# Every operand of TensorE at a multiple of 256 bytes, and the convolution mixer's end by halves of the tokens

## The chip, the cores and the metric

The kernel runs on one core of a Trainium2 chip. The metric is the time of one execution in microseconds (us) on the device. A core has a matrix engine (TensorE, PE in the profile), three engines that work on whole tiles (VectorE or DVE, ScalarE or ACT, GpSimd or POOL), SyncE (SP), which in this kernel issues nearly all transfers, an on-chip memory of 128 partitions (SBUF) and accumulators for PE in banks (PSUM).

## The reference

A trunk of four layers over 512 tokens of width 1024. Each layer has a token mixer (a Conformer convolution module, HGRN2, mLSTM, stick-breaking attention, in this order) and a gated feed-forward part (FFN) of inner width 2816:

```python
shift1, scale1, gate1, shift2, scale2, gate2 = split(silu(c) @ ada_w[i] + ada_b[i], 6)
h = x * (1 + scale1) + shift1
y = mixer(h)                                     # by layer
x = layer_norm(alpha * x + (1 + gate1) * y)
h = x * (1 + scale2) + shift2
x = layer_norm(alpha * x + (1 + gate2) * conv_ffn(h))

def conformer_conv_module(h):                    # mixer of layer 0
    u = glu(h @ w_pw1 + b_pw1)                   # 1024 -> 2048 -> 1024
    u = causal_dwconv(u, dw_w) + dw_b            # 31 taps, channel by channel
    u = silu(layer_norm(u, ln_g, ln_b))          # over the channels of a token
    return u @ w_pw2 + b_pw2
```

All is in 32-bit floats.

## The kernel before

**Products.** PE multiplies in a rounded 32-bit type (fp32r). To keep the precision each factor is split into a high and a low part, and a product is three matmuls: high by high, low by high, high by low. A weight tile `r_*` of 128x1024 comes by one transfer, ACT casts it to `wh_*` (L252), DVE subtracts to get `wl_*` (L254). Where an output is scaled by the row `gate` (1 + gate1), the raw weights are first multiplied by it on DVE (L242). A matmul has a stationary operand, which PE loads into its array ahead of time, and a moving one of up to 512 columns that streams through. In the products "up" (L282: `p_f`, `p_pw`, `p_mup`, ...) the weights are stationary and the activations `hh`, `hl` move. In the products "down" (L351: `p_d` of the FFN, `p_mdn`, `p_pw`, ...) the activations (`gr0h`, `muh`, `cuh`, ... and the low ones) are stationary and the weights move.

**Where tiles lie.** All tiles live in pools, stacked one behind another in each partition (4 bytes an element). Small tiles (a constant of 1 column, one of 8, statistics of 4 or 12 columns, modulation columns of 48) lie in the same pools as the large ones, and so decide at which byte each large tile begins. In the program before, the weight rings `wh`/`wl` and the activations `hh`/`hl` begin 192 bytes behind a multiple of 256. The FFN's down activations and those of the mLSTM begin 64 behind one, and so do the spare weight tiles with which the last three weight pairs of a down product are kept at once (`tail`, `spare`). The `hh_first` of the first product of the trunk begins 192 behind, its first weights (pool `start`) 224. The mLSTM's `ph`, `pl`, `wh_mv`, `wl_mv` begin at a multiple of 256.

**The conformer.** For each of 8 groups of 128 channels: two up products (`p_pw` L282, value and gate), a sigmoid, the product `upad`; `upad` goes to DRAM (`ud`) and comes back as four shifted copies `R`; 28 of the taps are matmuls (`pc` L681), the others run on DVE (`cv`); the sum (`cv` L689) is transposed to token-major (`ct` L653) and copied into `tm` (ACT), with statistics `cst` on DVE. Then comes the transition. All four blocks of 128 tokens are normalised, transposed back eight times (`cb` L703, 128x512), go through silu (L705, 512 tokens at a time), and are split into `cuh` and `cul` (L325, L326). Then the down product `p_pw` (L351) of 192 matmuls starts, with the gate rows (`gb` L445) just before it, and each bank of it is added to `X` on DVE (L585), which ends the sub-layer and leads to the FFN.

**The order.** PE's order is that of the code, here. On the other engines a list scheduler orders instructions by a priority: weight loads and splits are raised ahead. The modulation (`ada`, L207 and L208) is 48 units for a layer: a transfer of 512 KB on SP, and a multiply-and-sum of 128x1024 on DVE. `fill` puts units between the up products of the conformer (3 for each group), `flush` the rest. A transfer waits in SP's order until its tile is free, and all that stands behind it waits too.

Of the kernel before, what the change touches and what calls it, by code (L numbers as in the profile page):

```python
# [10 lines left out]
F32 = mybir.dt.float32  # L11
# [37 lines left out]
HEAD = 3  # L49

# [89 lines left out]

class Trunk:
    def __init__(self, ctx, tc, ins, out):
# [3 lines left out]
        self.const = E(tc.tile_pool(name="const", bufs=1))  # L146
        self.wp = E(tc.tile_pool(name="wp", bufs=2))
        self.xp = E(tc.tile_pool(name="xp", bufs=1))
        self.sp = E(tc.tile_pool(name="sp", bufs=2))
        self.ps = E(tc.tile_pool(name="ps", bufs=1, space=PSUM))  # L150
# [3 lines left out]
        self.ones = self.const.tile([P, 1], F32, name="ones")  # L154
# [3 lines left out]
        self.mhalf = self.const.tile([P, 8], F32, name="mhalf")  # L158
# [15 lines left out]

    def load_x(self):
        for t in range(NT):
            self.nc.sync.dma_start(out=self.X[t], in_=self.ins["x"][t * P:(t + 1) * P, :])
# [6 lines left out]
    def begin_layer(self, i):  # L184
# [5 lines left out]
        ab = self.sp.tile([P, 48], F32, tag="adab", name=f"adab{i}")  # L190
# [3 lines left out]
        ac = self.sp.tile([P, 48], F32, tag="adac", name=f"adac{i}")  # L194
# [286 lines left out]
    def mod_cols(self, i, which, prev):  # L481
# [10 lines left out]
        GB = self.sp.tile([P, 2 * KD], F32, tag="GB", name=f"GB{i}_{which}")  # L492
# [32 lines left out]
    def first_h(self, i, w=None, us=(), name=None):  # L525
# [5 lines left out]
        with tc.tile_pool(name="start", bufs=1, side="right", reuse_waits="tile") as st:  # L531
# [19 lines left out]
    def sub_end(self, ep, i, which, nxt, bias=None, gate=None, due=True):  # L551
# [22 lines left out]
        def evict(h, t, ps, partial=False):  # L574
# [7 lines left out]
            if h == 0:  # L582
                st[t] = self.sp.tile([P, 2, 6], F32, tag="st", bufs=4, name=f"st_{name}_{t}")
# [22 lines left out]
    def rstd(self, st, name):  # L606
        nc = self.nc
        mv = self.sp.tile([P, 4], F32, tag="mv", bufs=4, name=f"mv_{name}")
# [18 lines left out]
    def conformer(self, nxt):  # L627
# [9 lines left out]
        with tc.tile_pool(name="cf", bufs=1, reuse_waits="tile") as op, ExitStack() as es, \  # L637
                tc.tile_pool(name="cd", bufs=1, space=bass.MemoryType.DRAM) as dr:
# [4 lines left out]
            cf = es.enter_context(tc.tile_pool(name="cg", bufs=1, reuse_waits="tile"))  # L643
# [47 lines left out]
            self.flush(i, 40)  # L691
            self.apool = None
            es.close()
            cf = es.enter_context(tc.tile_pool(name="ch", bufs=1, reuse_waits="tile"))
# [12 lines left out]
            bias = cf.tile([P, D], F32, name="bpw2")  # L707
            nc.sync.dma_start(out=bias, in_=ins["bpw2"].broadcast_to([P, D]))
            gate, evict = self.sub_end(cf, i, 0, nxt, bias)
            act = self.ring(cf, us, "cu", keep=True)  # L710
            self.down(ins["pw2"], KD, act, "pw2", 2, evict, tail=TAIL, gate=gate,
                      spare=lambda tag, nm: cf.tile([P, D], F32R, tag="tw", bufs=4, name=nm))


    def hgrn(self, nxt):
# [4 lines left out]
        with tc.tile_pool(name="hg", bufs=1, reuse_waits="tile") as op, ExitStack() as es:  # L720
            og = [op.tile([P, T], F32, name=f"og{k}") for k in range(H)]
            ng = op.tile([P, 1], F32, name="hng")
            nc.sync.dma_start(out=ng, in_=ins["hng"])
            vs = es.enter_context(ExitStack())
            vp = vs.enter_context(tc.tile_pool(name="hv", bufs=1, side="right", reuse_waits="tile"))
            hp = es.enter_context(tc.tile_pool(name="hh", bufs=1, reuse_waits="tile"))
# [74 lines left out]
            def decay(hd, Q, F, K, G):  # L801
# [6 lines left out]
                ex = hp.tile([P, 3, NC], F32, tag="ex", bufs=2, name=f"ex{hd}")  # L808
# [16 lines left out]
            def mix(hd, stag, QP, KP, QD, KD_, dec):  # L825
# [48 lines left out]
                ms = hp.tile([P, 8], F32, tag="ms", bufs=2, name=f"ms{hd}")  # L874
# [56 lines left out]
            late["p"] = es.enter_context(tc.tile_pool(name="hw", bufs=1, side="right", reuse_waits="tile"))  # L931
# [5 lines left out]
    def mlstm(self, nxt):  # L937
# [7 lines left out]
        with tc.tile_pool(name="mx", bufs=1, reuse_waits="tile") as mp, \  # L945
                tc.tile_pool(name="md", bufs=1, space=bass.MemoryType.DRAM) as dr:
            xc = [mp.tile([P, T], F32, name=f"xc{m}") for m in range(NM)]
            with tc.tile_pool(name="ma", bufs=1, reuse_waits="tile") as ap:
                vd = [dr.tile([2, P, D], F32, name=f"mvd{h}") for h in range(H)]
                Sr = [ap.tile([P, 1280], F32, name=f"Sr{h}") for h in range(H)]  # L950
                self.psum(mm="012", at="34", sm="5", tr="67")
# [9 lines left out]
                msel = ap.tile([P, 8], F32, name="msel")  # L961
                nc.sync.dma_start(out=msel, in_=ins["msel"])
                bg = ap.tile([4, 2], F32, name="mbg")
# [25 lines left out]
                for hd in range(H):  # L989
# [4 lines left out]
                    for q in range(4):  # L994
# [12 lines left out]
                        bd = ap.tile([P, 32 + 4 * P], F32, tag="bd", bufs=1, name=f"bd{m}")  # L1007
# [52 lines left out]
                gb = ap.tile([P, 32 + 4 * P], F32, tag="bd", bufs=1, name="gb")[0:4, 0:T]  # L1060
# [92 lines left out]
    def stick(self, nxt):  # L1153
# [3 lines left out]
        with tc.tile_pool(name="so", bufs=1, reuse_waits="tile") as op, ExitStack() as es:  # L1157
# [134 lines left out]
            late["p"] = es.enter_context(tc.tile_pool(name="sf", bufs=1, reuse_waits="tile"))  # L1292
            self.psum(mm="234501", tr="67")
            for _ in dn:
                pass
# [85 lines left out]
```

## Time and profile before

| | |
|---|---|
| time, median of 3 runs | 2715.64 us (2715.63 to 2717.45) |
| the profiled execution | 2719.89 us, its span 2718.1 us |
| PE busy | 2620.6 us, 96% of the span, 13012 matmuls and transposes |
| DVE, ACT, POOL busy | 1991.0 us (73%), 1192.1 us (44%), 43.3 us (2%) |
| transfers | 352.66 MB, mean 130 GB/s |
| granted clock, mean | 0.987 |

The span is the profiled time without its start and end. PE's clock has two levels, 1.2 and 2.4 GHz; a granted clock of 1.00 is the upper one. A line of the profile such as L351 is a line of the kernel before. A matmul's duration in the profile overlaps with the next matmul, so the distance from one start to the next (the pitch) says what a matmul costs in a full stream, and a mean duration shows differences between groups. PE is full nearly everywhere. The stretch in which it is not is the conformer, up to 255 us, and its end above all.

### The profile page before, as it was taken

How to read it: one execution, taken by the hardware profiler on the slowest of the kernel's cores; microseconds unless marked ns; L12 is line 12 of the kernel's file. 1: busy time of each engine (PE TensorE's matmuls, PEld its weight loads, DVE VectorE, ACT ScalarE, POOL GpSimd, SP SyncE). 2: the span in 40 equal slices, each digit the busy share in tenths (PEclk: the TensorE clock that was granted, in tenths of full speed). 3: DMA queues.
4: the chain of work that ended last, by engine and by line, in shares of the span. 5: the costliest groups of instructions: out<-in, count | busy, mean ns of one | idle time of the engine just before them, and what ended most of it. 6: DMA issues, size and time to landing. Idle time of an engine off the chain costs nothing.

```text
span 2718.1 us, 33772 instructions
## 1 busy us (share of the span) xinstructions
PE 2620.6 (96%) x13012; PEld 2099.0 (77%) x13012; DVE 1991.0 (73%) x3051; ACT 1192.1 (44%) x1750; POOL 43.3 (2%) x80
## 2 busy tenths in 40 slices
PE   7979999999998999999999999999999999999998
PEld 5537888887876788888887778888887776888886
DVE  7558997775677799666766777898676577766676
ACT  3124433334774443334555543543434454543332
POOL 0000000000000000000000000000000000000000
PEclk9989999999998999999999999999999999999999
DMA  8843874232221386223222223675323311323232
GB/s 318 242 115 129 299 246 155 97 115 90 86 67 51 114 300 229 93 97 107 87 90 73 86 78 116 211 266 167 101 93 98 96 55 47 101 94 116 93 97 74
DMA packets 109529, 352.66 MB, mean 130 GB/s; under 512 B 12088, under 2 KB 22328, under 8 KB 109368
## 3 DMA queue, kind: packets, MB, share of 16 engines
q1 hardware_dynamic: 109368, 350.50, 39.2%
q8 instruction: 102, 1.67, 0.2%
q14 instruction: 59, 0.48, 0.1%
HBM read 341.96 MB, written 8.50 MB: 129 GB/s over the span
## 4 chain that ended last, share of the span: by engine, by line
PE 81%; DVE 8%; ACT 5%; DMA 3%; issue 2%; POOL 1%; SPq 0%; POOLq 0%; DVEq 0%; ACTq 0%
PE p_f L282 35%; PE p_d L351 16%; PE p_mup L282 6%; PE p_mdn L351 3%; PE p_hqf L282 2%; PE p_sqk L282 2%; PE p_pw L282 2%; PE p_hv L351 1%; PE p_sv L351 1%; PE p_pw L351 1%; DMA ada<-in_ada_dram 1%; PE ms L981 1%; ACT hf L515 1%; PE p_hg L282 1%; DMA r_swo<-in_swo_dram 1%
## 5 line engine op out<-in xcount | busy, mean ns | idle before, releaser
L282 PE MATMUL p_f<-hl,wh_f 128*128 128x512 f32 (+1 forms) x1504 | 565.4, 376 | 1.2 <-DVE hl L522 1.2
L282 PE MATMUL p_f<-hh,wl_f 128*128 128x512 f32 (+1 forms) x1504 | 564.8, 376 | 0.0
L282 PE MATMUL p_f<-hh,wh_f 128*128 128x512 f32 (+1 forms) x1504 | 564.1, 376 | 0.0
L252 ACT CAST wh_f<-r_f 128x1024 fp32r<-128x1024 f32 x176 | 185.0, 1052 | 340.8 <-PE p_f L282 308.3
L282 PEld LDWEIGHTS p_f<-hl,wh_f 128*128 128x128 f32 x1504 | 283.1, 188 | 53.0 <-DVE hl L522 1.6
L282 PEld LDWEIGHTS p_f<-hh,wh_f 128*128 128x128 f32 x1504 | 282.6, 188 | 52.2 <-ACT hh L521 0.9
L282 PEld LDWEIGHTS p_f<-hh,wl_f 128*128 128x128 f32 x1504 | 283.0, 188 | 51.0 <-issue 0.2
L254 DVE TENSOR_TENSOR wl_f<-r_f,wh_f 128x1024 fp32r<-128x1024 f32 x176 | 214.9, 1223 | 136.3 <-ACT wh_f L252 135.8
L208 DVE CUSTOM_DVE_ANT_0 ada<-ada,sbc,adab 128x1024 f32<-128x1024 f32 x192 | 243.4, 1278 | 8.3 <-DMA ada<-in_ada_dram 8.3
L1312 DVE SCALAR_TENSOR_TENSOR cv<-p_f,par,cv 128x511 f32<-128x511 f32 (+1 forms) x176 | 131.1, 745 | 1.4
L1312 DVE SCALAR_TENSOR_TENSOR cg<-p_f,par,cg 128x511 f32<-128x511 f32 (+1 forms) x176 | 131.1, 745 | 1.3
L242 DVE TENSOR_TENSOR r_d<-r_d,gate 128x1024 f32<-128x1024 f32 x88 | 107.5, 1222 | 27.7 <-DMA r_d<-in_fdn_dram 26.7
L1322 ACT ACTIVATE cg<-cg 128x512 f32<-128x512 f32 x88 | 55.4, 629 | 162.2 <-DVE cg L1312 162.2
L254 DVE TENSOR_TENSOR wl_d<-r_d,wh_d 128x1024 fp32r<-128x1024 f32 x88 | 107.4, 1221 | 11.3 <-ACT wh_d L252 11.3
L282 PE MATMUL p_mup<-hh,wh_mup 128*128 128x512 f32 (+1 forms) x280 | 108.4, 387 | 0.9 <-ACT hf L515 0.9
L282 PE MATMUL p_mup<-hh,wl_mup 128*128 128x512 f32 (+1 forms) x280 | 107.1, 382 | 0.0
L282 PE MATMUL p_mup<-hl,wh_mup 128*128 128x512 f32 (+1 forms) x280 | 106.6, 381 | 0.0
L252 ACT CAST wh_d<-r_d 128x1024 fp32r<-128x1024 f32 x88 | 92.3, 1048 | 20.0 <-PE p_f L282 16.0
L624 ACT ACTIVATE X<-X,mv 128x512 f32<-128x512 f32 x56 | 43.1, 810 | 82.0 <-DVE mv L612 82.0
L1310 ACT ACTIVATE cg<-p_f,par 128x512 f32<-128x512 f32 x88 | 68.1, 774 | 13.8 <-PE p_f L282 13.8
L351 PE MATMUL p_d<-wl_d,gr0h 128*128 128x512 f32 x176 | 69.6, 396 | 0.0
L351 PE MATMUL p_d<-wl_d,gr2h 128*128 128x512 f32 x176 | 69.6, 396 | 0.0
(469 smaller groups left out, 5619.5 us busy)
## 6 DMA issues: line engine op xcount, KB each, us to landing
ada<-in_ada_dram SPq DMA_DIRECT2D x192, 512.0 KB, 4.8
r_f<-in_fup_dram SPq DMA_DIRECT2D x176, 512.0 KB, 3.7
r_d<-in_fdn_dram SPq DMA_DIRECT2D x88, 512.0 KB, 3.3
r_mup<-in_mup_dram SPq DMA_DIRECT2D x32, 512.0 KB, 3.3
r_pw<-in_pw_dram SPq DMA_DIRECT2D x24, 512.0 KB, 6.9
r_hqf<-in_hqf_dram SPq DMA_DIRECT2D x16, 512.0 KB, 3.3
r_mdn<-in_mdn_dram SPq DMA_DIRECT2D x16, 512.0 KB, 3.3
r_sqk<-in_sqk_dram SPq DMA_DIRECT2D x16, 512.0 KB, 3.6
```

Of the source, the lines that this page charges most:

```text
L208: nc.vector.tensor_tensor_reduce(out=raw, in0=raw, in1=self.sbc, scale=1.0, scalar=ab[:, j:j + 1], op0=ALU.mult, op1=ALU.add, accum_out=ac ...
L242: nc.vector.tensor_tensor(out=r, in0=r, in1=gr, op=ALU.mult)
L252: nc.scalar.copy(hi, raw)
L254: nc.vector.tensor_tensor(out=lo, in0=raw, in1=hi.bitcast(F32), op=ALU.subtract)
L282: self.nc.tensor.matmul(ps[:, c0:c1], a, b[:, k, c0:c1], start=(n == 0), stop=(n == 3 * KD - 1))
L351: self.nc.tensor.matmul(bank, l[:, ts_], r, start=(kp == first and a == n == 0), stop=(kp == last and a == 1 and n == 2))
L515: nc.scalar.activation(out=hf[:, j, :], in_=ps[:, j * P:(j + 1) * P], func=AF.Identity, scale=G[:, k:k + 1], bias=B[:, k:k + 1])
L624: nc.scalar.activation(out=o[:, hs], in_=x[:, hs], func=AF.Identity, scale=mv[:, 2:3], bias=mv[:, 3:4])
L981: nc.tensor.matmul(ps[:, :n], a[:, c + sb * P:c + (sb + 1) * P], b[:, c + sb * P:c + T], start=(q == 0 and k == 0), stop=(q == 3 and k == 2))
L1310: nc.scalar.activation(out=o, in_=ps, func=AF.Identity, scale=w[2], bias=par[:, C_CONVB + m:C_CONVB + m + 1])
L1312: nc.vector.scalar_tensor_tensor(out=o[:, s:], in0=ps[:, :T - s], scalar=w[2 - s], in1=o[:, s:], op0=ALU.mult, op1=ALU.add)
L1322: nc.scalar.activation(out=cg, in_=cg, func=AF.Silu)
```

## The change

1. A wrapper `Lines` round the pools extends each tile to a multiple of 256 bytes of a partition, and the small tiles go to pools of their own (`few`, `sm`, `edge`, `hs`, `mk`) behind or beside the others, so that each tile that PE reads begins at a multiple of 256. That a later pool begins so follows from the pools before it. In the built program all operands named above begin at a multiple of 256. 2. The conformer's `fill` gives two units for each group instead of three, `flush` before the transition goes to 24, and 8 units (`ada_32` to `ada_39`) stand in the transition. 3. The gate rows are made before the last convolution ends. 4. The transition goes by halves of the tokens: tokens 0 to 255 first, with transposes, silu, casts and subtractions of 128x256, the casts by turns on ACT and DVE; the down product begins with its first three weight pairs on those tokens (`head`), then the same pairs on the others. The number of PE instructions is the same, 12094 in the program; ACT has 8 more, DVE 16 more.

```diff
+LINE = 256
+class Lines:
+    def __init__(self, pool):
+        self.pool = pool
+    def tile(self, shape, dtype, **kw):
+        n = int(np.prod(shape[1:]))
+        w = LINE // 4
+        if n % w == 0:
+            return self.pool.tile(shape, dtype, **kw)
+        t = self.pool.tile([shape[0], (n + w - 1) // w * w], dtype, **kw)[:, 0:n]
...
-        self.sp = E(tc.tile_pool(name="sp", bufs=2))
+        self.sp = E(self.pool(name="sp", bufs=2))
+        self.sm = E(tc.tile_pool(name="sm", bufs=2))
...
-        self.ones = self.const.tile([P, 1], F32, name="ones")
+        self.ones = few.tile([P, 1], F32, name="ones")
...
+    @contextmanager
+    def pool(self, **kw):
+        with self.tc.tile_pool(**kw) as p:
+            yield p if "space" in kw else Lines(p)
...
-        ab = self.sp.tile([P, 48], F32, tag="adab", name=f"adab{i}")
+        ab = self.sm.tile([P, 48], F32, tag="adab", name=f"adab{i}")
...
         # conformer
-                pg = self.up(ins["pw1"], KD + j, "pw1", fills=2)
+                pg = self.up(ins["pw1"], KD + j, "pw1", fills=1)
...
-            self.flush(i, 40)
+            self.flush(i, 24)
             self.apool = None
+            gate = self.gate_rows(op, i, 0)
             es.close()
...
-            for t in range(NT):
-                mv = self.rstd(st[t], f"cf{t}")
-                self.normalise(tm[:, t, :], tm[:, t, :], mv)
-            us = []
-            for j in range(KD):
-                ps = self.trbank(f"cb{j}")
-                for t in range(NT):
-                    nc.tensor.transpose(ps[:, t * P:(t + 1) * P], tm[:, t, j * P:(j + 1) * P], self.ident)
-                v = cf.tile([P, T], F32, tag="us", bufs=3, name=f"cs{j}")
-                nc.scalar.activation(out=v, in_=ps, func=AF.Silu, scale=lng(j), bias=lnb(j))
-                us.append(v)
+            ah, al = ([cf.tile([P, T], F32R, name=f"cu{z}{j}") for j in range(KD)] for z in "hl")
+            for s in range(2):
+                for t in (2 * s, 2 * s + 1):
+                    mv = self.rstd(st[t], f"cf{t}")
+                    self.normalise(tm[:, t, :], tm[:, t, :], mv)
+                hs = slice(2 * s * P, 2 * (s + 1) * P)
+                for j in range(KD):
+                    ps = self.trbank(f"cb{j}_{s}")
+                    for t in range(2):
+                        nc.tensor.transpose(ps[:, t * P:(t + 1) * P], tm[:, 2 * s + t, j * P:(j + 1) * P], self.ident)
+                    lo = cf.tile([P, 2 * P], F32, tag="us", bufs=4, name=f"cs{j}_{s}")
+                    nc.scalar.activation(out=lo, in_=ps[:, 0:2 * P], func=AF.Silu, scale=lng(j), bias=lnb(j))
+                    if j % 2:
+                        nc.vector.tensor_copy(ah[j][:, hs], lo)
+                    else:
+                        nc.scalar.copy(ah[j][:, hs], lo)
+                    nc.vector.tensor_tensor(out=al[j][:, hs], in0=lo, in1=ah[j][:, hs].bitcast(F32), op=ALU.subtract)
             bias = cf.tile([P, D], F32, name="bpw2")
             nc.sync.dma_start(out=bias, in_=ins["bpw2"].broadcast_to([P, D]))
-            gate, evict = self.sub_end(cf, i, 0, nxt, bias)
-            act = self.ring(cf, us, "cu", keep=True)
-            self.down(ins["pw2"], KD, act, "pw2", 2, evict, tail=TAIL, gate=gate,
-                      spare=lambda tag, nm: cf.tile([P, D], F32R, tag="tw", bufs=4, name=nm))
+            self.flush(i, 40, cf, 4)
+            gate, evict = self.sub_end(cf, i, 0, nxt, bias, gate=gate)
+            self.down(ins["pw2"], KD, lambda k, h: (ah[k], al[k]), "pw2", 2, evict, head=HEAD, tail=TAIL, gate=gate,
+                      spare=lambda tag, nm: cf.tile([P, D], F32R, tag="araw", bufs=4, name=nm))
```

The other hunks put the other pools into `Lines` and the other small tiles into the small pools; line numbers of the changed kernel are higher by 29 up to the conformer and by more behind it.

On PE, ahead of the down product of the conformer, the program before has this (`cb` are the transposes back, 32 of them behind the last convolution `pc7` and its transposes `ct7`):

```order
L703 MATMUL cb4_1334<-ident_70,tm_354 128x128 x4
L703 MATMUL cb5_1341<-ident_70,tm_354 128x128 x4
L703 MATMUL cb6_1348<-ident_70,tm_354 128x128 x4
L703 MATMUL cb7_1355<-ident_70,tm_354 128x128 x4
L445 MATMUL gb0_0_0_1370<-dg0_0_0_1365,onesr_74 128x512
L445 MATMUL gb0_0_1_1378<-dg0_0_1_1373,onesr_74 128x512
L351 MATMUL p_pw2_0_0_1390<-wh_pw2_0_1397,cuh0_0_1401 128x512
L351 MATMUL p_pw2_0_0_1390<-wh_pw2_0_1397,cul0_0_1402 128x512
L351 MATMUL p_pw2_0_1_1391<-wh_pw2_0_1397,cuh0_0_1401 128x512
L351 MATMUL p_pw2_0_1_1391<-wh_pw2_0_1397,cul0_0_1402 128x512
```

Now PE has, from the first gate row on:

```order
L474 MATMUL gb0_0_0_1267<-dg0_0_0_1262,onesr_85 128x512
L710 MATMUL pc7_1218<-R7_1209,lw7_1216 32x512 x28
L682 MATMUL ct7_1251<-ident_81,cv7_384 128x128 x4
L474 MATMUL gb0_0_1_1275<-dg0_0_1_1270,onesr_85 128x512
L735 MATMUL cb0_0_1312<-ident_81,tm_365 128x128
L735 MATMUL cb1_0_1319<-ident_81,tm_365 128x128
L735 MATMUL cb0_0_1312<-ident_81,tm_365 128x128
L735 MATMUL cb1_0_1319<-ident_81,tm_365 128x128
L735 MATMUL cb2_0_1326<-ident_81,tm_365 128x128 x2
L735 MATMUL cb3_0_1333<-ident_81,tm_365 128x128 x2
L380 MATMUL p_pw2_0_0_1473<-wh_pw2_0_1480,cuh0_1282 128x512
L380 MATMUL p_pw2_0_1_1474<-wh_pw2_0_1480,cuh0_1282 128x512
```

The first down matmul stood behind 32 transposes and both gate rows; it now stands behind 8 transposes of the first half, and the others are spread among the matmuls.

On DVE, before, the last convolution's sum (`cv7`) follows on the statistics of the group before it:

```order
L689 TENSOR_TENSOR cv6_372<-pc6_1103,cv6_372 128x512
L657 BN_STATS cst0_355<-tm_354 128x6
L657 BN_STATS cst1_356<-tm_354 128x6
L657 BN_STATS cst2_357<-tm_354 128x6
L657 BN_STATS cst3_358<-tm_354 128x6
L689 TENSOR_TENSOR cv7_373<-pc7_1231,cv7_373 128x512
```

Now seven operations on the weights of the down product (`gate`, `wl`) stand between the two on DVE:

```order
L686 BN_STATS cst3_369<-tm_365 128x6
L271 TENSOR_TENSOR r_pw2_0_1477<-r_pw2_0_1477,gate0_0_1261 128x1024
L271 TENSOR_TENSOR r_pw2_1_1484<-r_pw2_1_1484,gate0_0_1261 128x1024
L283 TENSOR_TENSOR wl_pw2_0_1482<-r_pw2_0_1477,wh_pw2_0_1480 128x1024
L283 TENSOR_TENSOR wl_pw2_1_1489<-r_pw2_1_1484,wh_pw2_1_1487 128x1024
L271 TENSOR_TENSOR r_pw2_2_1491<-r_pw2_2_1491,gate0_0_1261 128x1024
L271 TENSOR_TENSOR r_pw2_3_1570<-r_pw2_3_1570,gate0_0_1261 128x1024
L283 TENSOR_TENSOR wl_pw2_2_1496<-r_pw2_2_1491,wh_pw2_2_1494 128x1024
L718 TENSOR_TENSOR cv7_384<-pc7_1218,cv7_384 128x512
```

Weight tile 3 (`r_pw2_3`) takes the buffer of tile 0, of which there are three, after `wl_pw2_0` has been computed, and the last convolution's sum has moved behind it.

On SP, before, the transfers of two modulation units (`ada_38`, `ada_39`) stand just ahead of the last `ud`; now `ud` follows on the copies `R` of the group before it, and the eight units `ada_32` to `ada_39` stand behind the down product's sixth weight tile and ahead of its last two. On DVE these eight stand among the casts and subtractions of the two halves, the last two of them round the fourth `wl` of the down product; the bias rows (four of 128x1024 into `X`) follow behind the splits, and the first bank's addition to `X` behind those.

## Rows read from the trace of the kernel before

**Rows 1.** The page's chain of work that ended last, shares by engine.

```profile
PE 81%; DVE 8%; ACT 5%; DMA 3%; issue 2%; POOL 1%; SPq 0%; POOLq 0%; DVEq 0%; ACTq 0%
```

**Rows 2.** PE groups by form: out<-in, count, busy us, mean ns, idle before.

```profile
L282 PE MATMUL p_f<-hh,wh_f 128*128 128x512 f32 x1312 | 510.4, 389 | 0.0
...
L351 PE MATMUL p_d<-wl_d,gr0h 128*128 128x512 f32 x176 | 69.6, 396 | 0.0
...
L351 PE MATMUL p_d<-wh_d,gr3l 128*128 128x512 f32 x176 | 69.4, 394 | 0.0
...
L351 PE MATMUL p_mdn<-wl_mdn,muh 128*128 128x512 f32 x128 | 50.6, 396 | 0.0
```

**Rows 3.** PE in time, FFN 0 down: start us, duration, tail.

```profile
499.94 0.40 PE L351 MATMUL p_d<-wh_d,gr0h 128*128 128x512 f32 x1
...
607.07 0.40 PE L351 MATMUL p_d<-wl_d,gr0h 128*128 128x512 f32 x1
607.30 0.39 PE L351 MATMUL p_d<-wh_d,gr0h 128*128 128x512 f32 x1
607.53 0.39 PE L351 MATMUL p_d<-wh_d,gr0l 128*128 128x512 f32 x1
...
609.35 0.39 PE L351 MATMUL p_d<-wh_d,gr0h 128*128 128x512 f32 x1
```

**Rows 4.** PE in time, FFN 0 up.

```profile
299.64 0.39 PE L282 MATMUL p_f<-hh,wh_f 128*128 128x512 f32 x1
...
301.46 0.39 PE L282 MATMUL p_f<-hh,wl_f 128*128 128x512 f32 x1
```

**Rows 5.** PE in time, the first up-projection of the trunk.

```profile
38.81 0.39 PE L282 MATMUL p_pw<-hh_first,wl_pw 128*128 128x512 f32 x1
...
41.84 0.40 PE L282 MATMUL p_pw<-hl_first,wh_pw 128*128 128x512 f32 x1
...
51.38 0.39 PE L282 MATMUL p_pw<-hh_first,wl_pw 128*128 128x512 f32 x1
...
52.97 0.39 PE L282 MATMUL p_pw<-hh_first,wh_pw 128*128 128x512 f32 x1
```

**Rows 6.** PE in time, the mLSTM's value products.

```profile
1562.24 0.39 PE L1121 MATMUL mn<-wh_mv,ph 128*128 128x512 f32 x1
...
1565.86 0.39 PE L1121 MATMUL mn<-wl_mv,ph 128*128 128x512 f32 x1
```

**Rows 7.** Chain of waits around the conformer's end: start us, duration, what.

```profile
162.09 5.06 DMA ud<-upad
...
168.54 7.26 DMA R<-ud
...
175.94 8.32 PE pc L681 x56
...
185.12 0.64 PE ct L653 x4
...
192.18 1.28 ACT L705
...
203.88 1.15 DVE r_pw L242
...
206.14 33.20 PE p_pw L351 x138
```

**Rows 8.** Stretches: us, PE busy, PEclk, DMA share, GB/s.

```profile
170.00:190.00 20.00, 10.15 (x70) 0.75 0.31 68
190.00:210.00 20.00, 13.76 (x48) 0.67 0.03 7
```

**Rows 9.** What PE waited for from 60 to 262: total, times, longest.

```profile
PE ct L653 <- DVE cv L689: 6.5, 5, 2.2
...
PE pc L681 <- DMA R<-ud: 4.1, 1, 4.1
```

**Rows 10.** SP's issues before the last convolution's rows.

```profile
160.29 1.75 SPq L207 DMA_DIRECT2D ada<-in_ada_dram  x2
```

**Rows 11.** DVE groups by form, 50 to 256.

```profile
L208 DVE CUSTOM_DVE_ANT_0 ada<-ada,sbc,adab 128x1024 f32<-128x1024 f32 x24 | 30.2, 1279 | 1.9 <-DMA ada<-in_ada_dram 1.9
L254 DVE TENSOR_TENSOR wl_pw<-r_pw,wh_pw 128x1024 fp32r<-128x1024 f32 x17 | 20.3, 1218 | 1.0 <-ACT wh_pw L252 1.0
...
L242 DVE TENSOR_TENSOR r_pw<-r_pw,gate 128x1024 f32<-128x1024 f32 x8 | 9.6, 1221 | 0.1
...
L326 DVE TENSOR_TENSOR cul<-cs,cuh 128x512 fp32r<-128x512 f32 x8 | 5.2, 688 | 6.8 <-ACT cuh L325 6.8
L566 DVE SCALAR_TENSOR_TENSOR X<-X,bpw 128x1024 f32<-128x1024 f32 x4 | 4.9, 1219 | 0.0
```

More of the change, by code (lines that the diff above doesn't have):

```diff
@@ L138, in pack @@
     return {k: np.ascontiguousarray(v) for k, v in o.items()}
+class Lines:
[7 more added lines that the diff above has]
+        t = self.pool.tile([shape[0], (n + w - 1) // w * w], dtype, **kw)[:, 0:n]
+        if len(shape) == 2:
+            return t
+        names = "abcd"[:len(shape) - 1]
+        return t.rearrange(f"p ({' '.join(names)}) -> p {' '.join(names)}", **dict(zip(names, shape[1:])))
 class Trunk:
@@ L157, in __init__ @@
         nc.vector.tensor_copy(self.onesr, self.ones.broadcast_to([P, P]))
-        self.mhalf = self.const.tile([P, 8], F32, name="mhalf")
+        self.mhalf = few.tile([P, 8], F32, name="mhalf")
         nc.vector.memset(self.mhalf, -0.5)
@@ L193, in begin_layer @@
         nc.vector.tensor_scalar(out=ab[:, 32:48], in0=ab[:, 32:48], scalar1=1.0, scalar2=None, op0=ALU.add)
-        ac = self.sp.tile([P, 48], F32, tag="adac", name=f"adac{i}")
+        ac = self.sm.tile([P, 48], F32, tag="adac", name=f"adac{i}")
         self.adac[i] = ac
@@ L491, in mod_cols @@
         b = self.par[pi][:, C_PB + pw * KD:C_PB + (pw + 1) * KD]
-        GB = self.sp.tile([P, 2 * KD], F32, tag="GB", name=f"GB{i}_{which}")
+        GB = self.sm.tile([P, 2 * KD], F32, tag="GB", name=f"GB{i}_{which}")
         nc.vector.tensor_tensor(out=GB[:, :KD], in0=g, in1=sc, op=ALU.mult)
@@ L530, in first_h @@
         self.new_h("first")
-        with tc.tile_pool(name="start", bufs=1, side="right", reuse_waits="tile") as st:
+        with self.pool(name="start", bufs=1, side="right", reuse_waits="tile") as st:
             hl = []
@@ L582, in evict @@
             if h == 0:
-                st[t] = self.sp.tile([P, 2, 6], F32, tag="st", bufs=4, name=f"st_{name}_{t}")
+                st[t] = self.sm.tile([P, 2, 6], F32, tag="st", bufs=4, name=f"st_{name}_{t}")
             X = self.X[t]
@@ L607, in rstd @@
         nc = self.nc
-        mv = self.sp.tile([P, 4], F32, tag="mv", bufs=4, name=f"mv_{name}")
+        mv = self.sm.tile([P, 4], F32, tag="mv", bufs=4, name=f"mv_{name}")
         nc.vector.bn_aggr(out=mv[:, 0:2], in_=st.rearrange("p a b -> p (a b)"))
@@ L636, in conformer @@
         nd = CONV_W - CONV_PE
-        with tc.tile_pool(name="cf", bufs=1, reuse_waits="tile") as op, ExitStack() as es, \
-                tc.tile_pool(name="cd", bufs=1, space=bass.MemoryType.DRAM) as dr:
+        with self.pool(name="cf", bufs=1, reuse_waits="tile") as op, ExitStack() as es, \
+                self.pool(name="cd", bufs=1, space=bass.MemoryType.DRAM) as dr:
             par = op.tile([P, 288], F32, name="cpar")
@@ L930, in hgrn @@
             vs.close()
-            late["p"] = es.enter_context(tc.tile_pool(name="hw", bufs=1, side="right", reuse_waits="tile"))
+            late["p"] = es.enter_context(self.pool(name="hw", bufs=1, side="right", reuse_waits="tile"))
             self.psum(mm="345601", tr="27")
@@ L1059, in mlstm @@
                 gi, gf, ga = u4("gi"), u4("gf"), u4("ga")
-                gb = ap.tile([P, 32 + 4 * P], F32, tag="bd", bufs=1, name="gb")[0:4, 0:T]
+                gb = mk.tile([P, 32 + 4 * P], F32, tag="bd", bufs=1, name="gb")[0:4, 0:T]
                 for z, dst in ((0, gi), (1, gf)):
@@ L1145, in mlstm @@
                         nc.vector.tensor_tensor(out=xc[m], in0=xc[m], in1=sz, op=ALU.mult)
-            with tc.tile_pool(name="mb", bufs=1, reuse_waits="tile") as bp:
+            with self.pool(name="mb", bufs=1, reuse_waits="tile") as bp:
                 self.psum(mm="012345", tr="67")
@@ L1156, in stick @@
         HD = 64
-        with tc.tile_pool(name="so", bufs=1, reuse_waits="tile") as op, ExitStack() as es:
+        with self.pool(name="so", bufs=1, reuse_waits="tile") as op, ExitStack() as es:
             so = []
-            kp = es.enter_context(tc.tile_pool(name="sk", bufs=1, reuse_waits="tile"))
+            kp = es.enter_context(self.pool(name="sk", bufs=1, reuse_waits="tile"))
             v = [kp.tile([P, D], F32, name=f"sv{t}") for t in range(NT)]
@@ L1291, in stick @@
             es.close()
-            late["p"] = es.enter_context(tc.tile_pool(name="sf", bufs=1, reuse_waits="tile"))
+            late["p"] = es.enter_context(self.pool(name="sf", bufs=1, reuse_waits="tile"))
             self.psum(mm="234501", tr="67")
@@ L1301, in ffn @@
         up_w, dn_w = self.ins[f"fup{i}"], self.ins[f"fdn{i}"]
-        with tc.tile_pool(name=f"g{i}", bufs=1, reuse_waits="tile") as gp:
+        with self.pool(name=f"g{i}", bufs=1, reuse_waits="tile") as gp:
             gs = [gp.tile([P, T], F32, name=f"g{i}_{j}") for j in range(NF)]
@@ L1351, in trunk_kernel @@
             else:
-                with tc.tile_pool(name="start", bufs=1, reuse_waits="tile") as st:
+                with k.pool(name="start", bufs=1, reuse_waits="tile") as st:
                     k.flush(i, 48, st, 8)
```

48 lines of the change are left out of this document (26 added, 22 removed).

## The prediction

> **What bounds the kernel now.** I read the chain of work first. PE holds 81% of it, so the time is the sum of PE's matmuls plus the places where PE stands still [rows 1]. The change touches both.
>
> The first question is whether a matmul costs the same everywhere. PE's groups by form say no: matmuls of one shape, 128x512 with 128 partitions, have a mean of 389 ns in the FFN's up product and of 394 to 396 ns in the down products, in thousands of them [rows 2]. Durations overlap, so the cost is the distance between starts. In FFN 0's down product 462 matmuls start between 499.94 and 607.30: 107.36 us, 232.4 ns each. The next ones, from 607.53 to 609.35, are nine starts, eight steps, 227.5 ns each [rows 3]. Line, shape, clock and stationary operand are the same. What differs is that the weights of the last two pairs lie in the spare tiles: 64 bytes behind a multiple of 256, as the stationary activations do, whereas the ring's weights lie 192 behind. The up product, with both operands at 192, has 227.5 ns as well (eight steps from 299.64) [rows 4]. In the trunk's first product the activations lie at 192; while its weights begin at 224 a step is 233.1 ns (13 steps from 38.81), and when they come from the ring, at 192, it is 227.1 ns (seven steps from 51.38) [rows 5]. Three products, two of them with both pitches inside one line: I take it that a moving operand and the next stationary one at different places within 256 bytes cost a matmul some 5 ns.
>
> The second question is where PE stands still. From 170 to 190 us PE is busy 10.15 us of 20, from 190 to 210 it is 13.76 of 20, at granted clocks of 0.75 and 0.67 [rows 8]. That is the conformer's end. Its chain goes from the last `ud` (162.09) over the copies `R` (168.54), the last convolution (175.94) and its transposes (185.12) through a silu table load (192.18) and a gated weight (203.88) to the first down matmul at 206.14 [rows 7].
>
> **Alignment.** Nothing is added to an engine; equal begin for all operands takes the 4.9 ns (232.4 less 227.5) off each matmul that has unequal ones. The FFNs' down product is twelve groups of 176, each FFN 528 matmuls, 48 of them already with the spare weights: 4 x 480 = 1920. The mLSTM's is three groups of 128 [rows 2], less 48 likewise: 336. 2256 x 4.9 ns = 11.1 us. The out products of HGRN2 and stick-breaking are 384 more matmuls with other begins, 1.9 us at the same price. The first product has (51.38 - 38.81) / 0.2331 = 54 at 6.0 ns, 0.3 us. Sum 13.3 us. All of it lies on the path: those stages have no idle time ahead of a matmul [rows 2]. Bounds: none of it, if the begin isn't the cause; at the other end the groups' means, 395.5 against 389, 6.5 ns x 2694 = 17.5 us. I take 13.3, since the steps come from neighbouring matmuls.
>
> What speaks against it is a rule: the Trainium skill, "TensorE: Matmul & The Clock Gate", section "Step-by-step: what each phase is for", says that loading the next tile's weights does not take read bandwidth from the running matmul, because PE has a read port for each. By it the begin of the operands can't matter and this term is 0; by the steps of [rows 3] it is 13.3. The trace does not agree with the rule at 607.3 us, where nothing but the place of the weights changes; still the rule makes a rival (A).
>
> **The conformer up to its last transposes.** What there is to be had: PE waits 6.5 us for convolution sums and 4.1 us for the last `R` [rows 9]. One modulation unit less for each group (1.28 us of DVE, [rows 11]) unblocks DVE, and the last `ud` no longer stands behind two unit transfers (160.29, 1.75 us, and then the `ud` at 162.09) [rows 7, 10]. Against it stands DVE's new order: seven operations of 1.22 us on 128x1024 [rows 11], 8.5 us, are ahead of the last convolution's sum, and the sixth waits for a transfer that can start only when the third has freed its buffer. From the gate row on that is 3 x 1.22, a transfer of about 7.3 us (that of `R`, [rows 7], is the nearest), and 2 x 1.22: 13.4 us, against 8.3 us of convolution. So the sum comes 5 us behind the convolution, and the earlier `R` is mostly eaten. I take a gain of 2 us; bounds are a loss of 3 us (nothing gained ahead, part of the 5 lost) and a gain of 10.6 us less 0.6, the two waits nearly gone.
>
> **The transition.** Before, from the last `ct` to the first down matmul: 206.14 - 185.12 = 21.0 us. Now the first matmul needs the same statistics, two token blocks rather than four, the table load, one silu and one cast of half the size. The table load began 7.1 us behind the `ct` and takes 1.28 [rows 7]; two blocks fewer to scale are 1 to 2.5 us less of that (an estimate, from a third of the 7.1 at most), and silu and cast of 256 columns add 1 to 1.5 (twice 0.34 to 0.69, by the subtraction of 512 columns in [rows 11]). That makes 8 us, a saving of 13. The gates and casts that stood at 203.88 now run under the convolution.
>
> Of this, part comes back. 24 transposes now stand between the matmuls: about 0.11 us each by a quarter to a half of a 512-column step, 2.6 us. And DVE becomes the one that is late. Behind the `ct` it has 8 modulation units (10.2 us), five `wl` (6.1), four gatings (4.9), the bias (1.2 and 4 x 1.22), and 24 casts and subtractions of 256 columns, 0.34 to 0.69 us each (half of a 512-column one to all of it), 8.3 to 16.5 us. That is 36 to 44 us, ahead of the first addition to `X`, after some 5 us of statistics: 41 to 49 us behind the `ct`. PE comes to need a freed bank after 8 us, 125 matmuls of 0.2275 and the transposes: 39 us, and with a slow start like that of before (138 matmuls took 33.20 us instead of 31.4, [rows 7]) 41. It waits between nothing and 8 us; I take 1.5, near the low end, as a 512-column subtraction has 0.69 with its fixed part in it. So 13 - 2.6 - 1.5 = 9 us, bounds 2 (8 of wait, first matmul 2 later) and 12. The units cost DVE as much as before; their cover in the groups, PE's up products, is gone, and without the cover of the down product they would cost up to 10.2 us.
>
> **Sum.** 13.3 + 2 + 9 = 24.3 us. From the profiled execution, 2719.89, that is 2695.6; it ran 4.25 us above the median of 2715.64, so 2691 for the median. The rest of the program keeps its order.
>
> **The rivals.**
>
> A. The begin of the operands isn't what the steps follow, or PE's streams are bound elsewhere once they are equal, and the conformer alone counts: 2715.6 - 11 = 2705. For it: the rule above. Against it: the three pairs of steps [rows 3 to 5]. 0.12.
>
> B. DVE's queue takes the conformer's gain: the last sum comes 5 us late with no earlier `R`, and the banks 8 us late, so that 13 less 2.6, 8 and 3 leaves nothing. 2715.6 - 13 = 2702. For it: DVE has 36 to 44 us of work with a deadline of 41. Against it: the units' transfers fall into a stretch in which the transfer engines are 0.03 busy [rows 8]. 0.15.
>
> C. Slower: not the equality but the place counts. If a begin at a multiple of 256 is the slow one, where every operand now meets the same lines, the matmuls that had 227.5 rise. By the addresses of the built program some 6,800 of 128x512 have equal begins; at 232.4 they cost 33 us, the unequal ones gain nothing, and the conformer gives 11: 2738. It decides for slower from 24 us on, 3.6 ns a matmul, with the others' gain kept. For it: no large product had this place before. Against it: the mLSTM's value products lie at a multiple of 256 with both operands and have 226.3 ns (16 steps from 1562.24 to 1565.86) [rows 6]. 0.05.
>
> D. The wrapper doesn't do what it says for part of the operands, or the smaller gains cancel: no change. By the built program's addresses the operands are where they should be. 0.02.
>
> E. More than the sum: `R` comes early and the sum isn't late, 8 us more, 2683. 0.06 beside the forecast.
>
> **How the numbers follow.** The forecast has 0.60, around 2691 with its own range 2684 to 2699 (conformer 4 to 18, alignment 11 to 16). A and B reach to 2706 with part of their spread, E down to 2682; leaving out C, D and the outer tails, the range is 2681 to 2707. About 0.2%, 5.4 us, is what a measurement of this kernel can tell from none: forecast, E, and nearly all of A and B are faster by more, 0.90; same 0.04, from D and the end of B; slower 0.06, from C and from B with A.
>
> **What would show it.** Steps in FFN 0's down product of 227 to 228 ns from its first matmul on, and means of the `p_d` groups equal to those of `p_f`, show the alignment; 232 shows A; `p_f` above 389 shows C. In the conformer: the last `ud` issued directly when `upad` is there; first down matmul about 8 us behind the last `ct`, half-clock rows at its start; a wait of PE on `X` additions of 1 to 3 us near the end of the down product; `cv7` waiting on DVE for the gating of weight tile 3. FFN 0's first matmul should come some 11 us earlier than before. Wrong would be a conformer that ends within 3 us of before, a wait for banks of over 5 us, or the down steps unchanged.

## Result, and the profile after

The changed kernel takes 2690.41 us (median of 4 runs, 2685.80 to 2691.23) against 2715.64 us before: ratio 0.9900, 95% interval 0.9884 to 0.9915, that is 25 us faster. The forecast was 2691. A second set of runs beside others gave 2690.26, ratio 0.9895 (0.9879 to 0.9912), 30 us below the 2720.05 of before there. The profiled execution after is the fastest of the four (2685.80, span 2684.0), while the one of before was 4.25 us above its median. So the two traces differ by 34 us, and 9 of these are not the change. Below, stages are compared, not whole spans.

PE's groups by form after the change, for the groups of [rows 2]:

```profile
L311 PE MATMUL p_f<-hh,wh_f 128*128 128x512 f32 x1312 | 510.4, 389 | 0.0
...
L380 PE MATMUL p_d<-wl_d,gr0h 128*128 128x512 f32 x176 | 68.7, 391 | 0.0
...
L380 PE MATMUL p_d<-wh_d,gr3l 128*128 128x512 f32 x176 | 68.5, 389 | 0.0
...
L380 PE MATMUL p_mdn<-wl_mdn,muh 128*128 128x512 f32 x128 | 50.0, 391 | 0.0
```

The down products have come from 394 to 396 down to 389 to 391, the up product has stayed. PE in time (start, duration), the first matmul of FFN 0's down product and the one 462 matmuls on, the pair of [rows 3]:

```profile
484.25 0.39 PE L380 MATMUL p_d<-wh_d,gr0h 128*128 128x512 f32 x1
...
588.97 0.39 PE L380 MATMUL p_d<-wh_d,gr0h 128*128 128x512 f32 x1
```

104.72 us for 462 steps, 226.7 ns each, where it was 232.4. The conformer's end, in PE's timeline (in brackets the idle time ahead and who ended it):

```profile
158.86 7.48 PE L710 MATMUL pc<-R,lw 128*32 128x512 f32 x56
167.26 0.63 PE L682 MATMUL ct<-ident,cv 128*128 128x128 f32 x4 [0.92 <-DVE cv L718]
168.56 1.13 PE L474 MATMUL gb<-dg,onesr 128*128 128x512 f32 x2 [0.68 <-ACT tm L684]
169.62 6.22 PE L710 MATMUL pc<-R,lw 128*32 128x512 f32 x56
180.28 1.12 PE L682 MATMUL ct<-ident,cv 128*128 128x128 f32 x4 [4.44 <-DVE cv L718]
...
188.11 1.14 PE L735 MATMUL cb<-ident,tm 128*128 128x128 f32 x4 [1.66 <-ACT cs L737]
188.91 1.20 PE L380 MATMUL p_pw<-wh_pw,cuh 128*128 128x512 f32 x2
```

The last `ct` comes at 180.28 instead of 185.12 [rows 7], the first down matmul 8.63 us behind it instead of 21.0. The wait for `R` is gone; in its place stands the 4.44 us wait for the last sum. What DVE did in that time:

```profile
175.01 1.22 DVE L271 TENSOR_TENSOR r_pw<-r_pw,gate 128x1024 f32<-128x1024 f32 x1
177.26 1.23 DVE L271 TENSOR_TENSOR r_pw<-r_pw,gate 128x1024 f32<-128x1024 f32 x1 [1.03 <-DMA r_pw<-in_pw_dram]
178.40 1.22 DVE L283 TENSOR_TENSOR wl_pw<-r_pw,wh_pw 128x1024 fp32r<-128x1024 f32 x1
179.54 0.69 DVE L718 TENSOR_TENSOR cv<-pc,cv 128x512 f32<-128x512 f32 x1
```

The convolution was done at 175.84; its sum waited behind the gating of weight tile 3, which waited 1.03 us for its transfer, and behind one `wl`. The stretches of [rows 8] after:

```profile
170.00:190.00 20.00, 12.06 (x73) 0.71 0.60 210
190.00:210.00 20.00, 20.00 (x96) 0.95 0.40 132
```

From 190 us on PE is full, and the first matmul of FFN 0 comes 15.7 us earlier than before (before, then after):

```profile
254.81 0.51 PE L282 MATMUL p_f<-hh,wh_f 128*128 128x256 f32 x3
...
239.13 0.62 PE L311 MATMUL p_f<-hh,wh_f 128*128 128x256 f32 x3
```

In the stretch from 60 to 262 the profile shows no wait for a bank at all:

```profile
PE ct L682 <- DVE cv L718: 8.4, 4, 4.4
PE cb L735 <- ACT cs L737: 1.7, 1, 1.7
PE gb L474 <- ACT tm L684: 1.4, 2, 0.7
PE cb L735 <- DVE tm L650: 1.2, 1, 1.2
PE p_f L311 <- DVE hl L551: 0.7, 1, 0.7
```

### The profile page after: what moved, and what is told of

It reads as the page before. It is cut to its first block, busy times and chain, and to the rows that moved or that the text cites. A ratio compares the mean times of both kernels' runs of the same rounds, so it can differ in the third digit from the quotient of the medians.

```text
span 2684.0 us, 33793 instructions
## 1 busy us (share of the span) xinstructions
PE 2595.4 (97%) x13012; PEld 2090.5 (78%) x13012; DVE 1992.0 (74%) x3067; ACT 1192.9 (44%) x1758; POOL 43.8 (2%) x80
## 4 chain that ended last, share of the span: by engine, by line
PE 83%; DVE 8%; ACT 5%; DMA 1%; issue 1%; POOL 1%; SPq 0%; POOLq 0%; DVEq 0%; ACTq 0%
PE p_f L311 35%; PE p_d L380 16%; PE p_mup L311 6%; PE p_mdn L380 3%; PE p_sqk L311 3%; PE p_pw L311 3%; PE p_hqf L311 2%; PE p_hv L380 1%; PE p_sv L380 1%; PE pc L710 1%; PE p_hg L311 1%; PE ms L1019 1%; ACT hf L544 1%; PE tr L539 1%; PE mn L1158 1%
## 5 line engine op out<-in xcount | busy, mean ns | idle before, releaser
L283 DVE TENSOR_TENSOR wl_d<-r_d,wh_d 128x1024 fp32r<-128x1024 f32 x88 | 107.5, 1221 | 10.8 <-ACT wh_d L281 10.7
```

Of the source, the lines that this page charges most:

```text
L283: nc.vector.tensor_tensor(out=lo, in0=raw, in1=hi.bitcast(F32), op=ALU.subtract)
```

## Experiments

Two theories stood at the start: that unequal begins of PE's two operands cost the 5 ns, and that the conformer's two halves of the edit (units moved, transition halved) give 2 and 9 us. Ratios are to the kernel before, run beside them on the same chip (median there 2718.35 us for `align_only`, `conf_only`, `base64` and `mixed`, 2717.89 for `fills_only`, `halves_only`, `hold` and `hold_f4`, 2720.05 for `gate_early_hold`, `shift64`, `shift32` and the changed kernel once more).

### The two parts alone

Alignment with the old conformer (`align_only`: the old body of `conformer` with the new pools), and the new conformer with the old pools (`conf_only`). One line of the first:

```diff
-        with tc.tile_pool(name="cf", bufs=1, reuse_waits="tile") as op, ...   # align_only: old body, new pools
+        with self.pool(name="cf", bufs=1, reuse_waits="tile") as op, ...
```

> All operands at a multiple of 256 bytes, the conformer as before. Theory (a moving operand and the next stationary one that begin at different places within 256 bytes cost a matmul 5 ns): 13.3 us less than before, about 2702; FFN 0's down product 227 to 228 ns a step from its first matmul on. Rival A (the begin is not the cause): within 3 us of before, steps of 232.

> The conformer's new order alone, with tiles placed as before. Theory: 11 us less than before, about 2705 (8 to 16 by the trace of the changed kernel), the down steps unchanged at 232. Rival B (DVE's queue takes the conformer's gain): within 3 us of before. If the two parts are independent, this and the kernel with alignment alone add up to the whole change, 25 us.

Measured: 2701.75 us, 0.9939 (0.9926 to 0.9951), and 2704.04 us, 0.9942 (0.9930 to 0.9954). Each gives its part, 16.6 and 14.3 us below 2718.35. The product of the ratios, 0.9881, lies just below the first interval of the whole change (0.9884 to 0.9915) and inside the second (0.9879 to 0.9912): 31 us singly, 25 to 30 us together, which the noise does not tell apart. Steps in FFN 0's down product with alignment alone, 462 again:

```profile
498.02 0.39 PE L380 MATMUL p_d<-wh_d,gr0h 128*128 128x512 f32 x1
...
602.74 0.39 PE L380 MATMUL p_d<-wh_d,gr0h 128*128 128x512 f32 x1
```

226.7 ns; `conf_only` keeps 232.4 over its 462 steps. A and B are out: neither part is empty.

### Equal, or at a multiple of 256

`base64` moves every tile by 64 bytes (left pools by a longer first tile, right ones by a shorter one):

```diff
-        few.tile([P, 16], F32, name="edge_l")
+        self.edge_l = few.tile([P, 32], F32, name="edge_l")
-        self.edge = E(tc.tile_pool(name="edge", bufs=1, side="right")).tile([P, 56], F32, name="edge_r")
+        self.edge = E(tc.tile_pool(name="edge", bufs=1, side="right")).tile([P, 40], F32, name="edge_r")
```

> The changed kernel with every tile moved by 64 bytes: all operands begin 64 behind a multiple of 256, equal as before. Theory (equality counts): as the changed kernel, about 2690, steps of 227 to 228 in up and down products. Rival C (the place counts, a multiple of 256 is what helps): the gain of 13 us is lost, about 2704, or the steps differ from 227.

Measured: 2689.42 us, 0.9891 (0.9876 to 0.9907), as the changed kernel. The same two matmuls:

```profile
483.31 0.39 PE L380 MATMUL p_d<-wh_d,gr0h 128*128 128x512 f32 x1
...
588.03 0.39 PE L380 MATMUL p_d<-wh_d,gr0h 128*128 128x512 f32 x1
```

226.7 ns with all operands 64 behind a multiple. Rival C is out in the form that it has here, and so is the change's own wording: what counts is that the operands begin at the same place within 256 bytes, not that this place is 0. That 256 is the period has a sign too: in the changed kernel's built program the ring's weights begin 256 behind a multiple of 512 and the FFN's down activations at one, and its steps are 226.7 ns.

### Which step is long, and for which distance

`mixed` puts the high weights at 64, the low weights and the activations at 128; `shift64` and `shift32` put all ring weights at 64 or 96 and the activations at 128. All are the changed kernel with unused tiles put between the rings, as

```diff
+        self.wp.pool.tile([P, 16], F32, tag="pad1", bufs=1, name="pad1")
+        self.wp.pool.tile([P, D], F32R, tag="whi", bufs=WBUFS, name="wh_first")
+        self.wp.pool.tile([P, 16], F32, tag="pad2", bufs=1, name="pad2")
```

(`mixed`; in the others both rings lie between the two, the first of 64 or 96 bytes). `rc`, a small tile of the mLSTM, has one buffer in the three instead of two; the steps below are of FFN 0.

> The changed kernel with the high weights moved by 64 bytes, low weights and activations both by 128. Theory: a step is long only where the moving operand and the next stationary one differ: in an up product the two steps before a high weight take about 232, the one before a low weight 227; in a down product the two high-weight steps 232, the low-weight step 227. 6669 such pairs: about 33 us slower than the changed kernel, 2724. If 64 bytes are too little to matter: 227 throughout, about 2691.

> The changed kernel with all ring weights at 64 and all activations at 128 behind a multiple of 256. If any unequal begin costs the same, down steps of about 232 and up steps of about 230 to 232, 30 to 45 us slower than the changed kernel. If the cost grows with the distance (128 gave 232), down steps of about 229 to 230.

> As the one before with the weights at 96, 32 bytes before the activations. If any unequal begin costs the same: as with 64. If it grows with the distance: down steps of about 228 to 229, 5 to 15 us slower than the changed kernel.

Measured: 2719.12 us, 1.0004 (0.9993 to 1.0014); 2716.72 us, 0.9992 (0.9982 to 1.0003); 2740.29 us, 1.0079 (1.0059 to 1.0099). The weights 32 bytes from the activations make the kernel 50 us slower than equal begins (2690.26 beside it), 64 bytes 26 us, less than the 30 to 45 expected of an equal price. Steps, FFN 0's down product (462 steps) and 400 steps of its up product, of `shift64`:

```profile
300.07 0.39 PE L315 MATMUL p_f<-hh,wl_f 128*128 128x512 f32 x1
...
391.63 0.39 PE L315 MATMUL p_f<-hh,wh_f 128*128 128x512 f32 x1
...
487.43 0.39 PE L384 MATMUL p_d<-wh_d,gr0h 128*128 128x512 f32 x1
...
595.23 0.39 PE L384 MATMUL p_d<-wh_d,gr0h 128*128 128x512 f32 x1
```

and of `shift32`:

```profile
300.21 0.40 PE L315 MATMUL p_f<-hh,wl_f 128*128 128x512 f32 x1
...
393.54 0.40 PE L315 MATMUL p_f<-hh,wh_f 128*128 128x512 f32 x1
...
491.85 0.40 PE L384 MATMUL p_d<-wh_d,gr0h 128*128 128x512 f32 x1
...
599.64 0.39 PE L384 MATMUL p_d<-wh_d,gr0h 128*128 128x512 f32 x1
```

Down (weights move): 233.3 ns at 64 bytes and 233.3 at 32, 232.4 at 128 before. Up (activations move): 228.9 at 64, 233.3 at 32, 226.7 with equal begins. So the cost is 5.7 to 6.6 ns in the down product whatever the distance, 2.2 to 6.6 in the up product, and doesn't grow with the distance: of those tried the smallest is the worst. The trace of before had this already: 32 bytes the other way round (weights at 224, activations at 192) took 233.1 ns in the first up product [rows 5].

The expectation for `mixed` failed in its detail. By pairs the low-weight step should have been the short one in the down product. PE's groups by form there:

```profile
L383 PE MATMUL p_d<-wl_d,gr0h 128*128 128x512 f32 x176 | 70.2, 399 | 0.0
...
L383 PE MATMUL p_d<-wh_d,gr0l 128*128 128x512 f32 x176 | 69.9, 397 | 0.0
...
L383 PE MATMUL p_d<-wh_d,gr0h 128*128 128x512 f32 x176 | 69.1, 393 | 0.0
```

It is the longest, though it moves from 128 and all stationary operands begin at 128; 389 to 391 is what equal begins give. Durations overlap, but the starts say the same: over 510 steps of FFN 0's down product in this trace, the step from a low-weight matmul to the next is 236.9 ns on the mean, the one from `wh_d,gr0h` 229.9 and the one from `wh_d,gr0l` 234.9. The two longest are those behind which a moving operand with another begin follows. All three are above 226.7, and so are the three kinds of step in its up product (227.5, 228.7 and 230.5): the whole stream pays, not only the pair that differs. The kernel's total came near the forecast all the same (2719 for 2724), by other steps than it named.

### Units moved without halves, and halves without units moved

Both aligned. `fills_only` is the old transition with two units for each group and eight in the transition; `halves_only` has the new transition and early gate rows, with three units for each group:

```diff
-                pg = self.up(ins["pw1"], KD + j, "pw1", fills=2)   # fills_only; halves_only the reverse
+                pg = self.up(ins["pw1"], KD + j, "pw1", fills=1)
-            self.flush(i, 40)
+            self.flush(i, 24)
```

> Aligned, the conformer's transition as before, but two modulation units for each group instead of three and eight in the transition. Theory: the conformer's gain comes from two places, and this is the first: the last `ud` and the convolution sums no longer wait behind units, some 5 us; the eight units on DVE in an unhalved transition give part of it back. About 2699 (2 to 4 us below the aligned kernel with the old conformer, 2701.75). Rival: the units only change place, 2702 or above.

> Aligned, with the transition by halves and the early gate rows, but three modulation units for each group and none in the transition, as before. Theory: the transition's 9 us without the 2 to 5 us ahead of it: about 2693, 8 to 9 us below the aligned kernel with the old conformer. Rival: the halves bring nothing unless DVE and SP are freed ahead, 2700 or above.

Measured: 2693.32 us, 0.9913 (0.9900 to 0.9925), and 2701.27 us, 0.9943 (0.9929 to 0.9956). Both expectations were wrong: the moved units alone come 8.4 us below `align_only` (7 by the ratios), the halves alone bring nothing that the times show. The last `ct` and the first down matmul, of `align_only`, `fills_only` and `halves_only` in this order:

```profile
174.34 7.91 PE L710 MATMUL pc<-R,lw 128*32 128x512 f32 x56 [4.02 <-DMA R<-ud]
183.15 0.63 PE L682 MATMUL ct<-ident,cv 128*128 128x128 f32 x4 [0.90 <-DVE cv L718]
...
204.17 0.50 PE L380 MATMUL p_pw<-wh_pw,cuh 128*128 128x512 f32 x1 [2.73 <-ACT wh_pw L281]
```

```profile
165.70 0.63 PE L682 MATMUL ct<-ident,cv 128*128 128x128 f32 x4 [0.91 <-DVE cv L718]
166.26 6.22 PE L710 MATMUL pc<-R,lw 128*32 128x512 f32 x56
173.38 0.63 PE L682 MATMUL ct<-ident,cv 128*128 128x128 f32 x4 [0.90 <-DVE cv L718]
...
194.60 0.80 PE L380 MATMUL p_pw<-wh_pw,cuh 128*128 128x512 f32 x1 [2.46 <-ACT wh_pw L281]
```

```profile
167.58 8.45 PE L710 MATMUL pc<-R,lw 128*32 128x512 f32 x56 [4.95 <-DMA R<-ud]
...
190.13 1.11 PE L682 MATMUL ct<-ident,cv 128*128 128x128 f32 x4 [4.69 <-DVE cv L718]
...
198.76 1.20 PE L380 MATMUL p_pw<-wh_pw,cuh 128*128 128x512 f32 x2
```

Moved units bring the last `ct` 9.8 us forward (183.15 to 173.38) and leave the transition at 21.2 us; the eight units cost nothing there. Of the 9.8, 4.0 are the wait for `R`, 1.7 the last convolution (7.91 to 6.22 us, at a granted clock of 0.79 from 170 to 190 with `align_only`), and the rest was gained before: from 100 to 150 us PE is busy 46.50 us with `align_only` and 50.00 with `fills_only`. The halves cut the transition to 8.6 us, 12 us less, but with them the last `ct` comes 7.0 us later (183.15 to 190.13): 3.8 more of waiting for the sum (4.69 for 0.90), about 1.8 for the gate rows on PE, and an `R` wait that is still there, one group earlier. In the whole change the two meet at 180.28, and 6.9 us of the 9.8 are given back: 3.5 to the wait for the sum (4.44 for 0.90), 1.8 to the gate rows (from the `ct` before to the last convolution 2.36 us for 0.56), and the rest, 1.6 us, is mostly the convolution before the last, which ran 7.48 us in this execution for 6.22, at a granted clock of 0.91 from 150 to 170 for 1.00; in a second trace of the changed kernel it took 6.22. FFN 0's first matmul, at 252.83 with `align_only`, comes at 243.06 with the units moved, at 250.61 with the halves, and at 239.13 with both.

### The wait for the last sum taken away

`hold` queues weight tile 3's gating on DVE behind the last statistics and tile 2's behind the last sum; `hold_f4` puts four units back into the first four groups; `gate_early_hold` makes the gate rows after the sixth group:

```diff
+                if hold and h == 0 and kp in hold:                       # in down's load
+                    es.enter_context(self.tc.issue_after(hold[kp].ins))
...
+                      hold={2: cvsum, 3: stat},                          # conformer
-                pg = self.up(ins["pw1"], KD + j, "pw1", fills=1)         # hold_f4, and flush(i, 28)
+                pg = self.up(ins["pw1"], KD + j, "pw1", fills=2 if j < 4 else 1)
+                if j == KD - 3:                                          # gate_early_hold
+                    gate = self.gate_rows(op, i, 0)
```

> The changed kernel, with the third weight tile's gating held on DVE behind the last convolution's sum and the fourth's behind the last statistics. Theory (the last sum waits 4.4 us on PE's side because of the gating of weight tile 3 and its transfer): the last transposes come 3.6 us earlier, the whole 2 to 3.5 us faster than the changed kernel, about 2687. Rival: DVE's work up to the first bank sets the end of the conformer, and the time is that of the changed kernel, 2690.

> As the one before, and four of the eight modulation units back in the first four groups of the conformer. Theory: PE does not wait for banks in the changed kernel, so DVE's 5 us less in the transition bring under 1 us beyond the held one. Rival (DVE sets the end): 3 to 5 us beyond it.

> The held kernel with the gate rows made after the sixth group instead of after the last. Theory: the two gate matmuls and the copy they wait for stand between the last two convolutions and cost 3 us of PE there; the last convolution starts about 166.3 us instead of 169.2, and the whole is 2 to 3 us below the held kernel, about 2681. Rival: the `R` copies set the start of the last convolution and nothing is gained, 2684.

> The changed kernel once more beside the others of this call: 2690, some 3 us above the held one by their traces.

Measured: `hold` 2684.11 us, 0.9880 (0.9865 to 0.9895); `hold_f4` 2686.48, 0.9886 (0.9873 to 0.9900); `gate_early_hold` 2687.75, 0.9885 (0.9871 to 0.9900); the changed kernel again 2690.26. The last convolution, the last `ct` and the first down matmul of `hold`, and of the changed kernel in its second trace:

```profile
169.23 6.22 PE L714 MATMUL pc<-R,lw 128*32 128x512 f32 x56
176.26 0.66 PE L685 MATMUL ct<-ident,cv 128*128 128x128 f32 x4 [0.81 <-DVE cv L722]
...
186.16 1.20 PE L383 MATMUL p_pw<-wh_pw,cuh 128*128 128x512 f32 x2
```

```profile
167.52 6.22 PE L710 MATMUL pc<-R,lw 128*32 128x512 f32 x56
178.24 1.11 PE L682 MATMUL ct<-ident,cv 128*128 128x128 f32 x4 [4.50 <-DVE cv L718]
...
186.87 1.20 PE L380 MATMUL p_pw<-wh_pw,cuh 128*128 128x512 f32 x2
```

The wait falls from 4.44 (4.50 in the second trace) to 0.81 us. The two traces of the changed kernel stand 2 us apart at this place, so I count from the start of the last convolution: the `ct` follows after 7.0 us instead of 10.7, the first down matmul after 16.9 instead of 19.3, 2.4 us less. `hold` has the best median, but its interval overlaps with that of the changed kernel, so these 2.4 us are shown by the traces and not by the times; the 6 us between the medians (4 by the ratios) are more than the traces explain. Fewer units in the transition bring nothing more: nothing shows DVE setting its end. Moving the gate rows earlier missed: they then stand ahead of the convolution before the last, and the last one starts at 169.55 (169.23 held). The gate matmuls take PE's time there as well.

## Why the prediction was right

**Bound.** PE's steps and the conformer were where the time was, and 25 us or more came from these. That 2690.41 lies so close to 2691 is in part luck. Both parts were forecast too small: 13.3 us for 15 to 17 of alignment, and 11 for the conformer, where FFN 0's first matmul came 15.7 us earlier (2.0 of it with alignment alone, 252.83). The first measurement had a low median of before (2715.64), so that its 25 us lie below the 30 of the second set, though the two intervals overlap.

**Alignment: right, the size a little low.** The forecast took 4.9 ns from eight steps with starts rounded to 10 ns in [rows 3]; over 462 steps the difference is 232.4 - 226.7 = 5.7 ns. With that the three terms are 2256 x 5.7 = 12.9, 384 x 5.7 = 2.2 and 0.3: 15.4 us instead of 13.3, and `align_only` shows 16.6 (13 to 20 by its interval). The mean durations pointed at 6.5 and were not far off. The reason as the prediction put it, a moving operand against the next stationary one, held wherever the whole stream has one distance, with a price of 2.2 to 6.6 ns, but not inside a stream with several (`mixed`). The same instructions on the same engines took 226.7 or 233.3 ns by nothing but the tiles' places. The Trainium skill, "TensorE: Matmul & The Clock Gate", section "Step-by-step: what each phase is for", says that PE has two independent read ports, one for each operand, and that loading the next weights takes no read bandwidth from the running matmul. The steps do not agree with two reads that leave each other alone; the measurement decides.

**Ahead of the last transposes: right in mechanism, by the balance.** The forecast was 2 us; 4.7 were gained in `conf_only` (185.12 to 180.47 there), 2.9 between `align_only` and the whole change. The two sides were both there: DVE and SP freed of a unit in each group (9.8 us with `fills_only`, 4.0 of it the wait for `R`) and DVE's order, which delays the last sum. The 5 us that the forecast priced for the sum behind the convolution are 4.44 us of wait, 3.5 more than without it. Two terms of opposite sign are missing from the forecast: the 3.5 us that PE had lost between 100 and 150 us, and the 1.8 us of gate rows on PE between the last two convolutions.

**The transition: right, 2 us low.** First matmul 8.63 us behind the `ct` (forecast 8), and from the `ct` to FFN 0 10.8 us less than before (69.7 to 58.9), where the forecast had 9. This saving stands only beside the moved units: by the order in which the two are added, the halves are worth 2.2 us of FFN 0's start (250.61 for 252.83) or 3.9 (239.13 for 243.06), not 9, in single traces that differ by 1.7 us for one kernel (237.41 in the second trace of the changed one), mostly since their early gating delays the `ct` that the saving is counted from. So the forecast's split, 2 us ahead and 9 in the transition, describes where the time went, not which half of the edit earns it. The forecast then allowed 1.5 us for banks; there was no such wait, since a 256-column subtraction took about 0.38 us (0.76 for two) and a cast 0.29 on DVE, at the low end of the 0.34 to 0.69, and the first addition to `X` came at 220.82, 40.5 us behind the `ct`, where the forecast had 41 to 49.

**The rivals.** A fell with `align_only`, B with `conf_only`, D with the steps. C, that a begin at a multiple of 256 is the slow one, fell with the changed kernel's own 226.7 ns; `base64` rules out the reverse, that it is the fast one. B's mechanism is real all the same: DVE's queue holds the last sum for 4.4 us. It only does not eat the whole.

**What stays open.** Why unequal begins cost a step, inside PE or on its way to the memory; why 64 bytes cost the up product 2 ns and the down product 6; which matmul pays in a stream with several begins. The 2.4 us between the medians of `hold_f4` and `hold` lie within their intervals and ask for no cause.

## What to carry to other kernels

Where a matmul stream shows two step lengths for one shape, compare where the two operands' tiles begin within 256 bytes; equal begins were enough here, and it was small tiles in the same pools that made them differ. Measure a step over hundreds of matmuls, not eight. Work that is moved ahead in an engine's order is free only if it doesn't land ahead of the instruction that the critical engine waits for next (3.5 us here); a part of an edit tried alone can show nothing because another part pays for it.

## What was not expected of the hardware

A distance of 32 bytes between the operands' begins cost more (233.3 ns in both kinds of product, 50 us for the kernel) than one of 64 (228.9 and 233.3). And a matmul with equal begins in a stream with unequal ones was the longest of its group (mean 399 ns against 389 to 391, a step of 236.9 ns against 226.7).
